# A gated unit's products with the weights as the stationary operand, in a two-layer decoder trunk

## The chip, the cores and the metric

One core of one Trainium2 chip runs the whole program. The metric is the device time of one execution in microseconds, the median of three runs; lower is better.

## What is computed

Two layers on 256 tokens of 2048 features, all in float32. In each layer one input projection of the normalised stream gives seven parts of 2048 columns; the change concerns two of them, `glu_a` and `glu_b`.

```python
h = rms_norm(x, norm_g[layer])                        # x (1, 256, 2048)
proj = jnp.einsum("bsd,de->bse", h, w_in[layer])      # w_in (2048, 14336)
q, k, v, g_att, glu_a, glu_b, g_conv = jnp.split(proj, SPLIT_POINTS, axis=-1)
...
u = glu_a * jax.nn.sigmoid(glu_b)
u = jnp.pad(u, ((0, 0), (CONV_WIDTH - 1, 0), (0, 0)))
y = lax.conv_general_dilated(u, dw_kernel[:, None, :], window_strides=(1,), padding="VALID",
        dimension_numbers=("NWC", "WIO", "NWC"), feature_group_count=D_CONV) + dw_bias
y = jax.nn.silu(layer_norm(y, ln_g, ln_b))
conv = jnp.einsum("bsc,ce->bse", y, w_pw)
...
y = jnp.einsum("bse,ed->bsd", jnp.concatenate([att_y, conv_y], axis=-1), w_out[layer])
x = x + y
```

The depthwise convolution is 31 taps wide and causal over the tokens. The rest of a layer is attention of 16 heads, SiLU gates and two more normalisations.

## The kernel before, in words

**Large products.** The weights come as tiles of 256 rows by 512 columns (`raw`, four buffers). ACT rounds each to float32r (`whi`, L227), DVE takes the rest (`wlo`, L228), and the operand, the transposed activations, is held as such a pair too: `st_hi`, `st_lo`, 128 features by 256 tokens for each of 16 contraction tiles. A product of float32 accuracy is three products of float32r: hi by hi (L629), hi by lo (L630) and lo by hi (L631). A *step* is one weight tile: two contraction tiles by two halves of the tokens by three, 12 products. In each the 128 tokens of a half are the stationary operand, loaded ahead of it (engine PEld), and 512 columns of the weights are streamed. A *group* is eight steps: one chunk of 512 columns of one part, summed in two PSUM banks (`acc`), one for each half of the tokens. There are 80 groups, 640 steps, counted from 0. Per layer the groups go glu_b, glu_a, v, q, k for each of the four chunks j, then g_conv and g_att, and then o_att, pw and o_conv, four chunks each. Splits of weight tiles stand three steps ahead of their products in the program (`AHEAD`).

**Everything else** is put between the steps by `Filler`: a task is a generator that yields what its next slice needs (`Need`: engine times, PSUM banks, a condition), and a slice is put into the program once an estimate of how far each engine has got says that it fits. Each engine then works in program order. The last step of a group adds the task that takes its sums (`users`).

**The tasks of the gated unit.** The operand is not scaled by the tokens' rms; `rx`, a factor per token, comes in when the sums are taken, where tokens are on the partitions, so that it is a scale per partition.

- `ev_glu_b` (L292): ACT writes sigmoid(sums x rx) to `Dt[0]`, one instruction per half of the tokens (L295).
- `ev_glu_a` (L298): DVE multiplies sums by rx and by `Dt[0]` (L301). Then PE transposes the result by 128x128 blocks, eight of them, into two PSUM banks (`transposes`, L249 to L255), and ACT copies them to `uT`, features on the partitions (L309).
- `conv` (L314) works on `uT` on DVE, 124 instructions per chunk, followed by `layer_norm`, `ln_square` and `ln_silu`. The latter needs a factor per token along the free dimension: GpSimd spreads `rstd` to `rbc`, PE multiplies it by the identity (L380) and ACT copies it to `nmean` (L382). A plain f32 product has two records in the trace, one for each of its passes.

`x_square` (L281) computes `rx` from squares of the stream and sets the flag that `ev_glu_b` waits for in the first chunk.

Of the kernel before, what the change touches and what calls it, by code (L numbers as in the profile page):

```python
# [13 lines left out]
AF = mybir.ActivationFunctionType  # L14
ALU = mybir.AluOpType
# [8 lines left out]
NCH = 4  # L24
CH = 512
EPS = 1e-6
# Columns of the per-feature parameters: the taps by layer, then pairs by layer.
P_BIAS, P_LNG, P_LNB, P_ATT, P_CONV = (DEPTH * CW + DEPTH * i for i in range(5))
NPRM = DEPTH * (CW + 5)

# Weight tiles of [128, KS, CH]: a step is the products of one of them.
KS = 2
NSTEP = KT // KS
R_RAW, R_SPLIT = 4, 4
AHEAD = 3


class Need:
    """What the next slice of a task takes: time by engine (us, in the order in which its operations follow
    from one another), PSUM banks, and a condition that has to hold first."""  # L40

    def __init__(self, banks=0, when=None, **time):
        self.banks, self.when, self.time = banks, when, list(time.items())
# [3 lines left out]


class Filler:
    """Work beside the large products, in slices between their steps.  # L50

    A task is a generator that yields the Need of its next slice. The engines work in program order, so a
    slice is put into the program where its operands will about have been computed, by an estimate of how
    far each engine has got, and not where it would make the splits of the next weight tiles late."""

    HOP = 0.2

# [29 lines left out]
            self.banks.append((b, self.now[4]))  # L87

    def use(self, time, ready):
        """The time at which operations that follow from one another end, the first not before ready."""  # L90
        start = end = ready
        for e, cost in time:
            start = max(self.t[e], start)
            end = max(start + cost, end + 0.3)
            self.t[e] = end
            if e == "G":  # shares VectorE's port
                self.t["V"] = max(self.t["V"], start) + cost
                end += 1.0
            start += 0.45
        return end + self.HOP  # L100
# [43 lines left out]
def trunk(ctx: ExitStack, tc: tile.TileContext, x, norm_g, w_in, q_norm_g, k_norm_g, dw_kernel, dw_bias,  # L144
# [8 lines left out]
    def t(shape, name, dt=F32):  # L153
        return sb.tile(shape, dt, name=name)

    # Stationary operands by chunk of four contraction tiles, as exact sums hi + lo of float32r.
    st_hi = [[t([128, 4, SEQ], f"sthi{s}{c}", F32R) for c in range(4)] for s in range(2)]
    st_lo = [[t([128, 4, SEQ], f"stlo{s}{c}", F32R) for c in range(4)] for s in range(2)]
    Y = [t([128, 4 * SEQ], f"y{c}") for c in range(4)]
# [30 lines left out]
    sm_m = [t([128, 2], f"smm{i}") for i in range(4)]  # L190
    sm_r = [t([128, 2], f"smr{i}") for i in range(4)]
    rbc = t([128, 2, 128], "rbc")

    acc = [pp.tile([128, CH], F32, name=f"acc{i}") for i in range(4)]
    fill = Filler([pp.tile([128, CH], F32, name=f"ax{i}") for i in range(4)], dict(V=4.5, A=3.5), 5)

    xs = [dr.tile([SEQ, CH], F32, name=f"xs{c}") for c in range(NCH)]

# [1 line left out]
    groups = []  # L200
    for l in range(DEPTH):
        for j in range(NCH):
# [26 lines left out]
        halved[i] = fill.use([("A", 0.95), ("V", 1.14)], loaded[i])  # L229
        load(i + R_RAW)  # L230

# [1 line left out]
    ready = [[False] * 4 for _ in range(2)]  # a chunk of the operand is in place  # L233
    vacant = [[True] * 4 for _ in range(2)]  # all its products are in the program
    flags = set()

    def flag(*what):
        flags.add(what)

    def has(*what):  # L240
        return lambda: what in flags

    def rsqrt(r, ss, scale, n):
        """r = (ss * scale + EPS) ** -0.5 on [128, n]"""
        G.tensor_scalar(r, ss, scale, EPS, op0=ALU.mult, op1=ALU.add)
        G.tensor_tensor(r, r, half[:, :n], op=ALU.pow)

    def transposes(src, banks):
        """[128 tokens, 2, 4 x 128] -> two banks of [128, 2, 256 tokens]"""  # L249
        for b in range(2):  # L250
            for i in range(2):
                for tt in range(2):
                    e = (2 * b + i) * 128
                    T.transpose(banks[b][:, i * SEQ + tt * 128:i * SEQ + tt * 128 + 128],  # L254
                                src[:, tt, e:e + 128], ident)  # L255

    def to_stationary(src, s, c, gain):
        """Transposes a chunk and splits it, times a gain per feature."""
        yield Need(2, lambda: vacant[s][c], P=0.9)
        banks = [fill.bank(), fill.bank()]  # L260
        transposes(src, banks)
        yield Need(A=1.5, V=1.6)
        p = [b[:, i * SEQ:(i + 1) * SEQ] for b in banks for i in range(2)]
        for i in range(4):
            S.activation(st_hi[s][c][:, i], p[i], AF.Copy, scale=gain(i))  # L265
        for i in range(4):
            V.scalar_tensor_tensor(st_lo[s][c][:, i], p[i], gain(i), st_hi[s][c][:, i].bitcast(F32),  # L267
                                   op0=ALU.mult, op1=ALU.subtract)
        fill.free(*banks)
        filled(s, c)  # L270
# [3 lines left out]
        ready[s][c] = True  # L274

    def x_chunk(l, c):
        """A chunk of the residual stream, in A, becomes the next layer's operand."""
        yield from to_stationary(A[c], 0, c, lambda i: ng[:, l * KT + 4 * c + i:l * KT + 4 * c + i + 1])
        fill.add(x_square(l, c), 3, fill.now[4])

    def x_square(l, c):  # L281
        yield Need(A=1.4)
        for tt in range(2):
            S.activation(junk, A[c][:, tt], AF.Square, accum_out=ssx[:, tt, c:c + 1])  # L284
        flag("x", l, c)
        if all(("x", l, k) in flags for k in range(4)):
            yield Need(V=0.1, G=0.6)
            V.tensor_reduce(rsc, ssx, axis=mybir.AxisListType.X, op=ALU.add)
            rsqrt(rx, rsc, 1.0 / D, 2)
            flag("rx", l)  # L290

    def ev_glu_b(l, j, ps):  # L292
        yield Need(0, has("glu", l, j - 1) if j else has("rx", l), A=1.2)
        for tt in range(2):
            S.activation(Dt[0][:, tt], ps[tt], AF.Sigmoid, scale=rx[:, tt:tt + 1])  # L295
        flag("ev", l, "glu_b", j)

    def ev_glu_a(l, j, ps):  # L298
        yield Need(0, has("ev", l, "glu_b", j), V=1.4)
        for tt in range(2):  # L300
            V.scalar_tensor_tensor(Dt[0][:, tt], ps[tt], rx[:, tt:tt + 1], Dt[0][:, tt],  # L301
                                   op0=ALU.mult, op1=ALU.mult)
        flag("ev", l, "glu_a", j)
        yield Need(2, has("conv", l, j - 2) if j >= 2 else None, P=0.9)
        banks = [fill.bank(), fill.bank()]
        transposes(Dt[0], banks)
        yield Need(A=1.0)
        for b in range(2):
            S.activation(uT[j % 2][:, 2 * b:2 * b + 2, PAD:], banks[b].rearrange("p (c s) -> p c s", c=2), AF.Copy)  # L309
        fill.free(*banks)  # L310
        flag("glu", l, j)
        fill.add(conv(l, j), 5 + j, fill.now[4])

# [229 lines left out]
            yield from x_chunk(l + 1, j)  # L543
            nc.sync.dma_start(xs[j].rearrange("(t p) e -> p t e", p=128), A[j])

# [1 line left out]
    ng_in = t2[:DEPTH * KT, :128]  # L547
    S.dma_start(ng_in, norm_g.rearrange("l (k p) -> (l k) p", p=128))
    make_identity(nc, ident)
# [54 lines left out]
    fill.add(parameters(), 1, 45.0)  # L604
    split(0)

# [1 line left out]
    users = {"glu_b": ev_glu_b, "glu_a": ev_glu_a, "v": ev_v, "g_conv": ev_g_conv, "g_att": ev_g_att,  # L608
             "pw": ev_pw, "o_att": ev_o_att, "o_conv": ev_o_conv,
             "q": lambda l, j, ps: ev_qk(l, j, ps, "q"), "k": lambda l, j, ps: ev_qk(l, j, ps, "k")}  # L610
# [1 line left out]
    for i, (g, s) in enumerate(tiles):  # L612
        l, nm, j, _, _, _, st = groups[g]
        c = s * KS // 4
        fill.until(lambda: ready[st][c])
        if s == 0 and g >= 2:
            fill.until(has("ev", *groups[g - 2][:3]))
        for a in range(i + AHEAD if i else 1, i + AHEAD + 1):
            split(a)
        ps = [acc[(2 * g + tt) % 4] for tt in range(2)]  # L620
        hi, lo = whi[i % R_SPLIT], wlo[i % R_SPLIT]
        order = [(kk, tt) for kk in range(KS) for tt in range(2)]
        if s == NSTEP - 1:
            order.sort(key=lambda o: o[1])
        for kk, tt in order:
            k = s * KS + kk
            tok = slice(tt * 128, tt * 128 + 128)
            xh, xl = st_hi[st][c][:, k % 4, tok], st_lo[st][c][:, k % 4, tok]
            T.matmul(ps[tt], xh, hi[:, kk], start=(k == 0), stop=False)  # L629
            T.matmul(ps[tt], xh, lo[:, kk], start=False, stop=False)  # L630
            T.matmul(ps[tt], xl, hi[:, kk], start=False, stop=(k == KT - 1))  # L631
        fill.use([("P", 2.6)], halved[i])
        if i >= 2 and later:
            nc.sync.dma_start(*later.pop(0))
        if i == NSTEP:
            G.dma_start(mask, log_count)
            rope_tables(0)
        if s % 2 and j == NCH - 1 and nm in last[st]:
            ready[st][c], vacant[st][c] = False, True
        if s == NSTEP - 1:  # L640
            fill.add(users[nm](l, j, ps), 0, fill.t["P"])
            if nm == "o_att" and j == NCH - 1 and l + 1 < DEPTH:
                rope_tables(l + 1)
        fill.run()
# [8 lines left out]


def log_counts():
    """By query (in its tile of 128) and key: the log of how many branches attend it."""
    q = np.arange(SEQ)[:, None]
    k = np.arange(SEQ)[None, :]
    d = q - k
# [28 lines left out]
```

## Time and profile before

| | |
|---|---|
| median of 3 runs | 1864.1 us (1863.65 to 1865.67) |
| profiled execution, first to last instruction | 1863.1 us |
| PE busy | 1849.6 us (99%), 8525 matmuls |
| PEld busy | 1541.2 us (83%) |
| DVE busy | 1394.8 us (75%) |
| ACT busy | 988.8 us (53%) |
| POOL busy | 136.3 us (7%) |
| chain that ended last | PE 97%, DMA 2% |
| granted TensorE clock, mean | 0.998 |

The span is the profiled execution's time by its instructions; the runs' times also hold what lies around it, 1.0 us at the median. PE's busy time holds the fill of the array, so that products overlap in it: the start of one to the start of the next tells more than a length.

### The profile page before, as it was taken

What the parts mean: (1) busy time and instruction counts of PE and PEld (TensorE: products, weight loads), DVE (VectorE), ACT (ScalarE), POOL (GpSimd) and SP (SyncE); (2) the same over time, 40 slices, a digit from 0 to 9 for tenths busy, and PEclk for the clock granted to TensorE, in tenths of its full rate; (3) what the DMA queues carried; (4) which work ended last, traced back from release to release, by engine and by line L of the source; (5) the groups of instructions that cost most, each with busy time, mean ns of one, the idle gap of its engine ahead of it and who ended that gap; (6) DMA issues with size and microseconds to landing.
All of it is one profiled execution on the core that took longest, in us unless ns stands there. A gap on an engine that the chain in (4) does not pass through costs nothing.

```text
span 1863.1 us, 23820 instructions
## 1 busy us (share of the span) xinstructions
PE 1849.6 (99%) x8525; PEld 1541.2 (83%) x8525; DVE 1394.8 (75%) x2160; ACT 988.8 (53%) x1559; POOL 136.3 (7%) x153
## 2 busy tenths in 40 slices
PE   8999999999999999999999999999999999999999
PEld 6888888888888888888888888888888888888887
DVE  4778889888889885556558888797887998755554
ACT  5465564564654464445444655646556445644542
POOL 1110100100110140000000101002000102100000
PEclk9999999999999999999999999999999999999999
DMA  7765656656566676666666656566565666666564
GB/s 237 204 184 167 180 180 180 182 168 190 174 180 193 177 231 210 192 190 190 208 203 192 188 161 184 159 199 183 160 185 165 194 195 190 213 204 195 178 205 145
DMA packets 180880, 349.98 MB, mean 188 GB/s; under 512 B 11064, under 2 KB 11096, under 8 KB 180760
## 3 DMA queue, kind: packets, MB, share of 16 engines
q1 hardware_dynamic: 179176, 345.61, 61.2%
q0 software_dynamic: 960, 1.77, 0.5%
q8 instruction: 67, 1.10, 0.2%
q10 hardware_dynamic: 624, 1.07, 0.2%
q14 instruction: 53, 0.43, 0.1%
HBM read 344.21 MB, written 4.19 MB: 187 GB/s over the span
## 4 chain that ended last, share of the span: by engine, by line
PE 97%; DMA 2%; ACT 0%; SPq 0%; DVE 0%; issue 0%; ACTq 0%; DVEq 0%
PE acc L630 31%; PE acc L631 31%; PE acc L629 31%; PE ax L254 2%; DMA raw<-in_w_in 2%; PE ax L452 1%; PE ax L469 1%; PE ax L478 0%; PE ax L477 0%; PE ax L476 0%; PE ax L451 0%; ACT whi L227 0%; DVE wlo L228 0%; SPq L551 0%; ACT junk L284 0%
## 5 line engine op out<-in xcount | busy, mean ns | idle before, releaser
L228 DVE TENSOR_TENSOR wlo<-raw,whi 128x1024 fp32r<-128x1024 f32 x640 | 792.2, 1246 | 404.5 <-ACT whi L227 400.4
L227 ACT ACTIVATE whi<-raw 128x1024 fp32r<-128x1024 f32 x640 | 675.3, 1063 | 671.1 <-PE acc L631 471.5
L629 PE MATMUL acc<-whi,sthi 128*128 128x512 f32 x2560 | 1005.9, 393 | 2.7 <-ACT whi L227 2.7
L630 PE MATMUL acc<-wlo,sthi 128*128 128x512 f32 x2560 | 998.1, 390 | 0.8 <-DVE wlo L228 0.8
L631 PE MATMUL acc<-whi,stlo 128*128 128x512 f32 x2560 | 998.3, 390 | 0.0
L629 PEld LDWEIGHTS acc<-whi,sthi 128*128 128x128 f32 x2560 | 481.7, 188 | 100.9 <-ACT whi L227 3.1
L631 PEld LDWEIGHTS acc<-whi,stlo 128*128 128x128 f32 x2560 | 481.5, 188 | 101.0
L630 PEld LDWEIGHTS acc<-wlo,sthi 128*128 128x128 f32 x2560 | 481.8, 188 | 98.8 <-DVE wlo L228 1.1
L326 DVE SCALAR_TENSOR_TENSOR y<-ut,prm,y 128x256 f32<-128x256 f32 x960 | 411.1, 486 | 0.0
L414 POOL TENSOR_SCALAR qr<-qss 128x8 f32<-128x8 f32 x16 | 3.2, 197 | 692.1 <-ACT junk L411 692.1
L411 ACT ACTIVATE junk<-acc,rx 128x128 bf16<-128x128 f32 x128 | 47.1, 368 | 8.4 <-PE acc L631 4.8
L334 POOL TENSOR_TENSOR ysum<-ysum,y 128x256 f32<-128x256 f32 x30 | 31.8, 1058 | 237.1 <-DVE y L326 235.7
L421 ACT ACTIVATE d<-acc,qr 128x128 f32<-128x128 f32 x128 | 34.8, 383 | 18.0 <-POOL qr L416 18.0
L265 ACT ACTIVATE sthi<-ax,prm 128x256 fp32r<-128x256 f32 x64 | 25.1, 475 | 31.1 <-PE ax L254 31.1
L267 DVE SCALAR_TENSOR_TENSOR stlo<-ax,prm,sthi 128x256 fp32r<-128x256 f32 x64 | 26.5, 475 | 15.8 <-ACT sthi L265 15.8
L442 ACT ACTIVATE c<-ax 128x512 f32<-128x512 f32 x32 | 17.4, 597 | 33.6 <-PE ax L254 33.6
L465 ACT ACTIVATE sm<-sm,smm 128x128 f32<-128x128 f32 x64 | 28.2, 443 | 6.6 <-DVE smm L460 6.6
L362 POOL TENSOR_TENSOR ssum<-ssum,d 128x512 f32<-128x512 f32 x14 | 26.8, 1912 | 5.9 <-ACT d L355 5.0
L415 POOL TENSOR_TENSOR qr<-qr,half 128x8 f32<-128x8 f32 x16 | 26.3, 1642 | 1.3
L254 PEld LDWEIGHTS ax<-ident,d 128*128 128x128 f32 x192 | 22.4, 140 | 3.2
L254 PE MATMUL ax<-ident,d 128*128 128x128 f32 x192 | 24.9, 273 | 0.0
L411 ACT ACTIVATION_READ_ACCUMULATOR junk<-acc,rx 128x1 f32 x128 | 24.7, 193 | 0.0
(106 smaller groups left out, 669.4 us busy)
## 6 DMA issues: line engine op xcount, KB each, us to landing
raw<-in_w_in SPq DMA_DIRECT2D x448, 512.0 KB, 3.9
raw<-in_w_out SPq DMA_DIRECT2D x128, 512.0 KB, 4.6
raw<-in_w_pw SPq DMA_DIRECT2D x64, 512.0 KB, 4.6
a<-in_x SPq DMA_DIRECT2D x8, 512.0 KB, 5.7
xs<-a SPq DMA_DIRECT2D x4, 512.0 KB, 6.0
a<-xs SPq DMA_DIRECT2D x4, 512.0 KB, 6.5
out<-a SPq DMA_DIRECT2D x4, 256.0 KB
out<-a ACTq DMA_DIRECT2D x4, 256.0 KB, 5.1
```

The source lines that it names most:

```text
L227: S.activation(hi, a, AF.Copy)
L228: V.tensor_sub(wlo[i % R_SPLIT], a, hi.bitcast(F32))
L254: T.transpose(banks[b][:, i * SEQ + tt * 128:i * SEQ + tt * 128 + 128], src[:, tt, e:e + 128], ident)
L326: V.scalar_tensor_tensor(y[:, c], u[:, c, k:k + SEQ], w[:, c, l * CW + k:l * CW + k + 1], y[:, c], op0=ALU.mult, op1=ALU.add)
L334: G.tensor_add(ysum, ysum, y[:, c])
L362: G.tensor_add(ssum, ssum, half_sq)
L411: S.activation(junk[:, :DH], ps[tt][:, h * DH:(h + 1) * DH], AF.Square, scale=rx[:, tt:tt + 1], accum_out=qss[:, tt, h:h + 1])
L421: S.activation(n[:, tt, h * DH:(h + 1) * DH], ps[tt][:, h * DH:(h + 1) * DH], AF.Copy, scale=qr[:, tt, h:h + 1])
L465: S.activation(s[:, cs], s[:, cs], AF.Exp, bias=m[:, tt:tt + 1], scale=-1.0, accum_out=lsum[:, tt:tt + 1])
L629: T.matmul(ps[tt], xh, hi[:, kk], start=(k == 0), stop=False)
L630: T.matmul(ps[tt], xh, lo[:, kk], start=False, stop=False)
L631: T.matmul(ps[tt], xl, hi[:, kk], start=False, stop=(k == KT - 1))
```

## The change

In the groups of glu_b and glu_a the operands change places. A block of 128x128 weights is the stationary operand and all 256 tokens are streamed, so that a step has two contraction tiles by four blocks of features by three, 24 products of 256 columns. The sums have features on the partitions; a bank holds two blocks of 256 tokens. The factor `rx` now lies along the free dimension, so `x_square` makes `rxb` of it, spread over all partitions, by a copy on GpSimd, two products with the identity and a copy on ACT; `rxb` uses the buffer of `nmean`. `ev_glu_b` multiplies by `rxb` on DVE and takes the sigmoid on ACT in one instruction of 1024 columns; `ev_glu_a` multiplies sums by the gate, and then by `rxb` straight into `uT`. The transposes and their copies go. Other groups are as before.

```diff
     rbc = t([128, 2, 128], "rbc")
+    rxb = nmean
...
             rsqrt(rx, rsc, 1.0 / D, 2)
             flag("rx", l)
+            G.tensor_copy(rbc, rx[:, :, None].to_broadcast([128, 2, 128]))
+            yield Need(1, P=0.5)
+            ps = fill.bank()
+            for tt in range(2):
+                T.matmul(ps[:, tt * 128:tt * 128 + 128], rbc[:, tt], ident, start=True, stop=True)
+            yield Need(A=0.4)
+            S.activation(rxb, ps[:, :SEQ], AF.Copy)
+            fill.free(ps)
+            flag("rxb", l)
...
     def ev_glu_b(l, j, ps):
-        yield Need(0, has("glu", l, j - 1) if j else has("rx", l), A=1.2)
-        for tt in range(2):
-            S.activation(Dt[0][:, tt], ps[tt], AF.Sigmoid, scale=rx[:, tt:tt + 1])
+        yield Need(0, has("glu", l, j - 1) if j else has("rxb", l), V=1.4)
+        d = Dt[0].rearrange("p t (i s) -> p t i s", i=2)
+        for b in range(2):
+            V.tensor_mul(d[:, b], ps[b].rearrange("p (i s) -> p i s", i=2), rxb[:, None, :].to_broadcast([128, 2, SEQ]))
         flag("ev", l, "glu_b", j)
+        yield Need(A=1.1)
+        S.activation(Dt[0], Dt[0], AF.Sigmoid)
+        flag("sig", l, j)
 
     def ev_glu_a(l, j, ps):
-        yield Need(0, has("ev", l, "glu_b", j), V=1.4)
-        for tt in range(2):
-            V.scalar_tensor_tensor(Dt[0][:, tt], ps[tt], rx[:, tt:tt + 1], Dt[0][:, tt],
-                                   op0=ALU.mult, op1=ALU.mult)
+        yield Need(0, has("sig", l, j), V=1.4)
+        for b in range(2):
+            V.tensor_mul(Dt[0][:, b], ps[b], Dt[0][:, b])
         flag("ev", l, "glu_a", j)
-        yield Need(2, has("conv", l, j - 2) if j >= 2 else None, P=0.9)
-        banks = [fill.bank(), fill.bank()]
-        transposes(Dt[0], banks)
-        yield Need(A=1.0)
-        for b in range(2):
-            S.activation(uT[j % 2][:, 2 * b:2 * b + 2, PAD:], banks[b].rearrange("p (c s) -> p c s", c=2), AF.Copy)
-        fill.free(*banks)
+        yield Need(0, has("conv", l, j - 2) if j >= 2 else None, V=1.25)
+        V.tensor_mul(uT[j % 2][:, :, PAD:], Dt[0].rearrange("p t (i s) -> p (t i) s", i=2),
+                     rxb[:, None, :].to_broadcast([128, 4, SEQ]))
...
+        if nm in FEATURE_MAJOR:
+
+            order = [(kk, f) for kk in range(KS) for f in range(4)]
+            if s == NSTEP - 1:
+                order.sort(key=lambda o: o[1] // 2)
+            for kk, f in order:
+                k = s * KS + kk
+                fs = slice(f * 128, f * 128 + 128)
+                o = ps[f // 2][:, f % 2 * SEQ:f % 2 * SEQ + SEQ]
+                xh, xl = st_hi[st][c][:, k % 4], st_lo[st][c][:, k % 4]
+                first = k == 0 and f % 2 == 0
+                T.matmul(o, hi[:, kk, fs], xh, start=first, stop=False, skip_group_check=True)
+                T.matmul(o, lo[:, kk, fs], xh, start=False, stop=False, skip_group_check=True)
+                T.matmul(o, hi[:, kk, fs], xl, start=False, stop=(k == KT - 1), skip_group_check=True)
+        else:
...
```

`FEATURE_MAJOR` is ("glu_b", "glu_a"); under `else` stand the products as they were. Lines of the changed program are its own: L645 to L647 are the products of the gated unit's groups there, L656 to L658 those of the others, L231 the split on DVE, L309, L318 and L321 the three steps of the gated unit on DVE, L312 the sigmoid.

Three places show the order of instructions. First PE, in the first step of the first group, one contraction tile of the program before (`acc` is the PSUM bank, the number behind a name its buffer):

```order
L629 MATMUL acc0_153<-whi0_93,sthi00_65 128x512
L630 MATMUL acc0_153<-wlo0_97,sthi00_65 128x512
L631 MATMUL acc0_153<-whi0_93,stlo00_73 128x512
L629 MATMUL acc1_154<-whi0_93,sthi00_65 128x512
L630 MATMUL acc1_154<-wlo0_97,sthi00_65 128x512
L631 MATMUL acc1_154<-whi0_93,stlo00_73 128x512
```

and in the changed program, from the second block of features of the first bank to the first block of the second bank:

```order
L645 MATMUL acc0_153<-sthi00_65,whi0_93 128x256
L646 MATMUL acc0_153<-sthi00_65,wlo0_97 128x256
L647 MATMUL acc0_153<-stlo00_73,whi0_93 128x256
L645 MATMUL acc1_154<-sthi00_65,whi0_93 128x256
L646 MATMUL acc1_154<-sthi00_65,wlo0_97 128x256
L647 MATMUL acc1_154<-stlo00_73,whi0_93 128x256
```

Where three products of 512 columns filled a bank's share of a contraction tile, three of 256 now fill half of it, and three more like them, for the bank's other block of features, stand beside them: twelve instead of six in all.

Second PE, in the group of v of the second chunk, around the transposes of the gated unit's result (`d0`), before:

```order
L630 MATMUL acc3_156<-wlo0_97,sthi00_65 128x512
L631 MATMUL acc3_156<-whi0_93,stlo00_73 128x512
L254 MATMUL ax2_159<-ident_116,d0_107 128x128 x4
L254 MATMUL ax3_160<-ident_116,d0_107 128x128 x4
L629 MATMUL acc2_155<-whi1_94,sthi00_65 128x512
```

and in the changed program:

```order
L657 MATMUL acc3_156<-wlo0_97,sthi00_65 128x512
L658 MATMUL acc3_156<-whi0_93,stlo00_73 128x512
L656 MATMUL acc2_155<-whi1_94,sthi00_65 128x512
L657 MATMUL acc2_155<-wlo1_98,sthi00_65 128x512
L658 MATMUL acc2_155<-whi1_94,stlo00_73 128x512
```

The eight transposes are gone and the next step follows directly.

Third DVE, where the sums of glu_a of the second chunk are taken (`acc0`, `acc1`), between splits of weight tiles and taps of the first chunk's convolution, before:

```order
L228 TENSOR_TENSOR wlo2_99<-raw2_91,whi2_95 128x1024
L301 SCALAR_TENSOR_TENSOR d0_107<-acc0_153,rx_133,d0_107 128x512
L301 SCALAR_TENSOR_TENSOR d0_107<-acc1_154,rx_133,d0_107 128x512
L228 TENSOR_TENSOR wlo3_100<-raw3_92,whi3_96 128x1024
L326 SCALAR_TENSOR_TENSOR y0_81<-ut0_101,prm_124,y0_81 128x256 x4
```

and in the changed program:

```order
L231 TENSOR_TENSOR wlo2_99<-raw2_91,whi2_95 128x1024
L318 TENSOR_TENSOR d0_107<-acc0_153,d0_107 128x512
L318 TENSOR_TENSOR d0_107<-acc1_154,d0_107 128x512
L321 TENSOR_TENSOR ut1_102<-d0_107,nmean_126 128x4x256
L231 TENSOR_TENSOR wlo3_100<-raw3_92,whi3_96 128x1024
```

One instruction of 1024 columns stands ahead of the next split that did not stand there before; two more (L309) stand at the end of each glu_b group. On DVE the last split of the layer norm's result in the first layer stands behind the split of weight tile 248, before it stood behind that of tile 236; the first group of pw begins with tile 256.

## Rows read from the trace of the kernel before

**Rows 1.** The page: span, and busy time of the engines.
```profile
span 1863.1 us, 23820 instructions
...
PE 1849.6 (99%) x8525; PEld 1541.2 (83%) x8525; DVE 1394.8 (75%) x2160; ACT 988.8 (53%) x1559; POOL 136.3 (7%) x153
```

**Rows 2.** The page: the chain that ended last, share of the span by engine.
```profile
PE 97%; DMA 2%; ACT 0%; SPq 0%; DVE 0%; issue 0%; ACTq 0%; DVEq 0%
```

**Rows 3.** Groups by line and shape, PE: xcount | busy us, mean ns.
```profile
L629 PE MATMUL acc<-whi,sthi 128*128 128x512 f32 x2560 | 1005.9, 393 | 2.7 <-ACT whi L227 2.7
```

**Rows 4.** Stretches of one group: length, busy PE, PEld, DVE, ACT, POOL, clock, DMA, GB/s.
```profile
34.34:63.79 29.45, 26.04 (x109) 20.70 (x108) 12.80 (x12) 12.23 (x13) 9.54 (x17) 0.88 0.76 214
...
205.09:226.85 21.76, 21.76 (x98) 18.02 (x96) 18.57 (x29) 10.16 (x14) 1.66 (x2) 1.00 0.66 192
...
300.67:323.33 22.66, 22.66 (x106) 18.85 (x104) 21.04 (x37) 10.17 (x11) 0.00 (x0) 1.00 0.66 193
```

**Rows 5.** PE in order of time, steady: start us, length us, engine, line, instruction.
```profile
1637.41 0.39 PE L629 MATMUL acc<-whi,sthi 128*128 128x512 f32 x1
...
1640.13 0.39 PE L629 MATMUL acc<-whi,sthi 128*128 128x512 f32 x1
```

**Rows 6.** PE in order of time, plain f32 products of attention.
```profile
151.21 0.38 PE L451 MATMUL ax<-c,c 128*128 128x128 f32 x2
151.43 0.60 PE L452 MATMUL ax<-c,c 128*128 128x256 f32 x2
151.86 0.38 PE L451 MATMUL ax<-c,c 128*128 128x128 f32 x2
```

**Rows 7.** PEld in order of time: loads beside two-column matmuls, then a large product's.
```profile
674.28 1.08 PEld L370 LDWEIGHTS ax<-ones,ssum 128*128 128x128 f32 x8
675.28 0.19 PEld L629 LDWEIGHTS acc<-whi,sthi 128*128 128x128 f32 x1
675.39 0.19 PEld L630 LDWEIGHTS acc<-wlo,sthi 128*128 128x128 f32 x1
```

**Rows 8.** PE in order of time, the nine products after twelve transposes (L469).
```profile
158.13 0.40 PE L630 MATMUL acc<-wlo,sthi 128*128 128x512 f32 x1
...
160.22 0.39 PE L630 MATMUL acc<-wlo,sthi 128*128 128x512 f32 x1
```

**Rows 9.** PE in order of time around its wait at 42 us.
```profile
42.28 0.39 PE L631 MATMUL acc<-whi,stlo 128*128 128x512 f32 x1
45.31 0.50 PE L629 MATMUL acc<-whi,sthi 128*128 128x512 f32 x1 [2.65 <-ACT whi L227]
46.58 0.79 PE L630 MATMUL acc<-wlo,sthi 128*128 128x512 f32 x1 [0.76 <-DVE wlo L228]
...
47.59 0.63 PE L629 MATMUL acc<-whi,sthi 128*128 128x512 f32 x1
...
51.43 0.63 PE L629 MATMUL acc<-whi,sthi 128*128 128x512 f32 x1
```

**Rows 10.** Two stretches of one us, columns as in rows 4.
```profile
7.00:8.00 1.00, 0.28 (x3) 0.06 (x1) 0.30 (x1) 1.00 (x3) 0.00 (x0) 1.00 1.05 408
...
49.00:50.00 1.00, 1.00 (x4) 0.81 (x3) 0.47 (x1) 0.99 (x1) 0.12 (x1) 0.50 1.08 307
```

**Rows 11.** PE in order of time: four passes of the broadcast of the layer norm.
```profile
683.34 0.40 PE L631 MATMUL acc<-whi,stlo 128*128 128x512 f32 x1
683.57 0.61 PE L380 MATMUL ax<-ident,rbc 128*128 128x128 f32 x4
...
684.25 0.39 PE L630 MATMUL acc<-wlo,sthi 128*128 128x512 f32 x1
```

**Rows 12.** Groups by line and shape, DVE and ACT.
```profile
L301 DVE SCALAR_TENSOR_TENSOR d<-acc,rx,d 128x512 f32<-128x512 f32 x16 | 11.3, 744 | 0.2 <-PE acc L631 0.2
...
L390 DVE TENSOR_TENSOR y<-y,nmean 128x1024 f32<-128x1024 f32 x8 | 9.4, 1219 | 0.0
...
L309 ACT ACTIVATE ut<-ax 128x512 f32<-128x512 f32 x16 | 8.7, 596 | 17.3 <-PE ax L254 17.3
```

More of the change, by code (lines that the diff above doesn't have):

```diff
@@ L35 @@
 AHEAD = 3
+FEATURE_MAJOR = ("glu_b", "glu_a")
 class Need:
@@ L621, in trunk @@
         hi, lo = whi[i % R_SPLIT], wlo[i % R_SPLIT]
[L622 to L631, printed above, removed]
+        if nm in FEATURE_MAJOR:
[12 more added lines that the diff above has]
+        else:
+            order = [(kk, tt) for kk in range(KS) for tt in range(2)]
+            if s == NSTEP - 1:
+                order.sort(key=lambda o: o[1])
+            for kk, tt in order:
+                k = s * KS + kk
+                tok = slice(tt * 128, tt * 128 + 128)
+                xh, xl = st_hi[st][c][:, k % 4, tok], st_lo[st][c][:, k % 4, tok]
+                T.matmul(ps[tt], xh, hi[:, kk], start=(k == 0), stop=False)
+                T.matmul(ps[tt], xh, lo[:, kk], start=False, stop=False)
+                T.matmul(ps[tt], xl, hi[:, kk], start=False, stop=(k == KT - 1))
         fill.use([("P", 2.6)], halved[i])
```

## The prediction

> **What bounds the kernel now.** I read the page first, then the chain of waits, then the stretches of single groups, and last the instructions of TensorE in order of time. The page has PE busy for 1849.6 of 1863.1 us [rows 1], and the chain is PE for 97% of the span [rows 2]. A stretch of one group shows why: 96 large products take 21.76 us with nothing between them, and at most 18.6 us of DVE and 10.2 of ACT lie beside them [rows 4]. So what PE issues is the time, and every ns of a large product's pitch counts: there are 3 x 2560 of them [rows 3]. PE's one real wait is near the start, at 42 us [rows 9], where a weight tile comes late; outside it, work on other engines costs nothing unless PE is made to wait for it.
>
> The mean of 393 ns [rows 3] is a length with the fill of the array in it. What counts is the pitch: twelve products from one L629 to the next take 2.72 us, 226.7 ns each [rows 5].
>
> **The change part by part.** *Large products.* In 16 of the 80 groups (two of the gated unit, four chunks, two layers) a step's 12 products of 512 moving columns become 24 of 256, each with its own load of 128x128. That is 128 steps, 1536 products at 226.7 ns = 348.2 us before and 3072 products at a pitch p after. The columns streamed are as many as before; the loads are twice as many. No large product in the trace has 256 columns, so p has to be bounded.
>
> From below: beside matmuls of two columns the loads are all that is left. The eight loads of L370 and the next take 1.00 us, of which the first waits 0.227 for a large product; (1.00 - 0.227)/7 = 0.110, and the next two loads, of large products, are 0.11 apart [rows 7]. So p is at least 111 ns, however well loads hide; now a load of 111 hides under 227.
>
> What 256 columns take themselves: after the wait at 42 us PE ran at the granted clock 0.50 [rows 10], the level of 1.2 GHz, and nine products took 3.84 us, 426.7 each [rows 9], which is 512 columns at 1.2 GHz and nothing else. At 2.4 GHz the same would be 213.3, but the pitch is 226.7: 13.3 ns are added that the slower array does not show. Plain f32 products, which take twice the time per column, show 215 for 256 columns and 110 for 128 [rows 6], so 2 to 3 ns. The 13.3 ns thus belong to feeding the array at full rate. If they go with the columns, 256 of them take 113.3. If they go with each product and its load, they take 106.7 + 13.3 = 120.0. I take 120.0, because the extra is not a steady rate: behind a run of transposes nine products take 2.09 us, 232.2 each [rows 8], 18.9 over the array's 213.3, until the old pitch returns. An excess that depends on how the loads stand to the products looks like load and stream disturbing each other, and each product still has one load. The upper end is the undisturbed array plus that larger excess, 106.7 + 18.9 = 125.6.
>
> The Trainium skill, "TensorE: Matmul & The Clock Gate", Part 2, step 1, speaks for the change here: TensorE has two independent read ports, and loading the next weights steals nothing from the running stream; its section on the back-to-back gap gives N/2.4 + 2.5 ns, which is 215.8 for 512 columns and 109.2 for 256. The trace has 226.7 where that gives 215.8, so for these operands it disagrees. By the page the loads of 111 would set the pitch, and this term would be a gain of 7.2 us.
>
> At p = 120.0: 3072 x 0.120 = 368.6, so **+20.5 us**. Ends: 341.0 (-7.2) and 385.8 (+37.6).
>
> *Transposes.* Eight blocks of eight transposes go away, since the sums already have features on the partitions. Such a block stands in a group of v, 22.66 against 21.76 us [rows 4]: 0.90 each, **-7.2 us**. Their eviction on ACT, two of 596 ns each [rows 12], was beside.
>
> *Broadcast of the norm.* Per layer GpSimd copies rx to rbc, PE multiplies it by the identity, ACT copies it out. The layer norm does the same on L380: from the product ahead to the one behind 0.91 us where two pitches are 0.45 [rows 11], so 0.46 each, **+0.9 us**. It stands behind the first group, when rx is long there.
>
> *The wait at the start.* PE stands from the last product of step 10 (42.28) to 45.31, and then 0.76 us more for the low half; the tile was late from memory [rows 9], its load being released by ACT and DVE, not by PE. What PE does slower ahead of that point shortens the wait: 11 steps x (24 x 0.120 - 2.72 = 0.16) + 0.46 = **-2.2 us**. The clock fell behind this wait, and some 14 products up to 52.7 us ran at 426.7 instead of 226.7. An idle of 0.7 us in a stretch with PE busy 0.28 near the start left the clock at 1.00 [rows 10]. With the first idle cut to about half a us, I expect the clock to stay: 14 x 0.200 = **-2.8 us**. If it falls all the same, that term is 0.
>
> *DVE and ACT.* Per chunk the two L301 (0.744) become four products with PSUM and one of 1024 columns (1.219) [rows 12]: 4 x 0.744 + 1.219 - 1.488 = 2.7 us more on DVE, 22 us in all; ACT loses two evictions. The sigmoid now waits for DVE, and behind it in ACT's queue stand splits of weight tiles; these are three steps ahead of PE, 8.2 us, and DVE's two products and the sigmoid are under 4. In the new order the layer norm's last split comes 12 weight tiles later on DVE than before, still ahead of the tile that needs it. DVE had 21.0 of 22.7 us busy in a middle stretch [rows 4], but that includes the convolution, which is put where there is room. I cost this at nothing; the cover is those three tiles and, for the convolution, the eight tiles from the last split (tile 248) to the first group of pw (tile 256).
>
> Sum: 20.5 - 7.2 + 0.9 - 2.2 - 2.8 = +9.2, so a span of 1872.3. The runs' median of 1864.1 lies 1.0 above the span, which I add: **1873.3 us**. A measurement can tell about 0.2%, 3.7 us.
>
> **The rivals.** *Columns carry the excess, or loads alone set the pitch.* The place is the same stream. At p = 113.3 the first term is 0, the wait is shortened by 0.5 only, the clock falls as before, and the span changes by -7.2 + 0.9 - 0.5 = -6.8: 1857.3. At p = 111 it is 7.2 less, about 1850; this is what the Trainium skill's page named above leads to. The case decides against my forecast below p = 116 or so. For it: the pitch settles at exactly 17/16 of the array's time, which a feed with a fixed rate could give. Against: 232.2 behind transposes [rows 8]. Chances 0.16 and 0.06.
>
> *Load and stream slow each other both.* Now loads fill half of the stream's time; with p = 120 they would fill nearly all of it. If a load of 111 is itself stretched by 18.9, p = 130: 399.4, +51.2 and, with the other terms (the wait then shortened by all of its 3.4), about 1903. For it: rows 8 show that phases matter. Against: at the settled pitch the load leaves room. Chance 0.08.
>
> *DVE makes PE wait.* If all 22 us came to the path, about 1895. The cover above speaks against it: 0.03.
>
> *The change does not do what it says.* The order shows 24 products per step and no transposes there: excluded.
>
> **How the numbers follow.** Forecast 0.67, of which 0.07 with p between 114 and 117.5 lies within 0.2%. Faster: 0.16 + 0.06 = 0.22. Within: 0.07 and a little of the first rival's upper side, 0.09. Slower: the rest, 0.69. The forecast's own range: p = 117 gives about +0.2, p = 125.6 gives 37.6 - 7.2 + 0.9 - 3.4 - 2.8 = +25.1, so 1865 to 1890. The range reaches down to 1857 to hold the column case; it leaves out loads alone (0.06), p of 130 (0.08), and a few per cent above: 1857 to 1890.
>
> **What would show it.** The steps of the gated unit's groups at 2.88 us instead of 2.72, with products 120 ns apart; a group of the gated unit without other work at 23.0 us instead of 21.8; groups of v at 21.8; the stretch from 34 to 64 us with the clock near 1.00 and a wait under 1 us ahead of the first product; DVE near 1416 us and no wait of PE in the rest. The prediction is wrong if the pitch is 113 or less, or over 126, or if PE waits for DVE or ACT in the middle.

## The result, and the profile after

The changed kernel takes 1876.2 us (median of 4 runs, 1875.1 to 1878.7) against 1864.35 (4 runs): a ratio of 1.0065, 95% interval 1.0053 to 1.0077, 11.9 us more. The forecast was 1873.3, slower, within 1857 to 1890.

The page of the changed kernel answers to [rows 1, 2]:

```profile
span 1874.9 us, 26793 instructions
...
PE 1862.2 (99%) x10005; PEld 1616.6 (86%) x10005; DVE 1419.9 (76%) x2184; ACT 981.4 (52%) x1537; POOL 144.6 (8%) x155
...
PE 97%; DMA 2%; ACT 0%; DVE 0%; SPq 0%; issue 0%; ACTq 0%; DVEq 0%
```

PE is still busy for 99% of the span and 97% of the chain. Its instructions have grown from 8525 to 10005: 1536 products more, 64 transposes fewer, 8 passes of the broadcast more. The answer to [rows 5] is in order of time on PE; 24 products lie between these two rows:

```profile
1062.03 0.28 PE L645 MATMUL acc<-sthi,whi 128*128 128x256 f32 x1
...
1064.91 0.28 PE L645 MATMUL acc<-sthi,whi 128*128 128x256 f32 x1
```

2.88 us for 24 products is 120.0 ns each, the value that the prediction took, and a step of the gated unit's groups costs 2.88 us instead of 2.72. The stretches of groups answer to [rows 4]; they are, in order, the second group of the program, the first group of the third chunk, a group of glu_a with nothing between its products, and the group of v behind it (columns as there):

```profile
36.52:65.55 29.03, 26.36 (x208) 25.56 (x206) 13.86 (x14) 11.47 (x13) 8.63 (x13) 0.94 0.70 202
251.92:279.66 27.74, 27.74 (x230) 27.53 (x228) 20.71 (x45) 19.19 (x49) 3.08 (x3) 1.00 0.53 163
...
970.27:993.32 23.05, 23.05 (x195) 23.05 (x194) 11.07 (x11) 10.70 (x10) 0.00 (x0) 1.00 0.64 184
993.32:1015.10 21.78, 21.78 (x98) 18.02 (x97) 20.10 (x34) 9.18 (x9) 0.00 (x0) 1.00 0.65 190
```

The undisturbed group has gone from 21.76 to 23.05 us, with PEld busy from end to end; the group of v from 22.66 to 21.78, since its transposes are gone. The first group of the third chunk, with attention between its products, takes 27.74 us, 1.2 more rather than 1.28; its row of before:

```profile
249.51:276.06 26.55, 26.55 (x133) 22.44 (x132) 20.52 (x45) 19.40 (x48) 3.08 (x3) 1.00 0.53 169
```

The second group has 29.03 us where [rows 4] have 29.45, with a mean clock of 0.94 for 0.88.

What PE waited for, longest in total, after the loads of the first 8 us (which are as before): line, releaser, us in total, times, longest:

```profile
PE ax L596 <- DMA y<-in_conv_out_g: 1.6, 1, 1.6
PE acc L646 <- DVE wlo L231: 1.1, 2, 0.9
```

The two waits for the weight tile, 2.65 and 0.76 us [rows 9], have become one of 0.9 in the same place, and a new one of 1.6 has come up behind it, for the last row of the per-feature parameters, which PE transposes at L596. In order of time on PE:

```profile
46.68 0.39 PE L646 MATMUL acc<-sthi,wlo 128*128 128x256 f32 x1 [0.88 <-DVE wlo L231]
...
58.50 0.28 PE L647 MATMUL acc<-stlo,whi 128*128 128x256 f32 x1
60.36 0.60 PE L596 MATMUL ax<-ident,y 72*128 72x72 f32 x6 [1.58 <-DMA y<-in_conv_out_g]
...
61.27 0.42 PE L645 MATMUL acc<-sthi,whi 128*128 128x256 f32 x1
...
63.19 0.41 PE L645 MATMUL acc<-sthi,whi 128*128 128x256 f32 x1
```

From the first of the last two rows to the second, nine products take 1.92 us, 213 ns each: 256 columns at the half clock, 213.3, and again no excess. The clock had fallen behind the new wait, for 3.4 us (columns as in [rows 4]):

```profile
61.10:64.40 3.30, 3.30 (x18) 3.30 (x17) 2.32 (x3) 0.10 (x1) 1.51 (x3) 0.50 0.94 250
```

That is the profiled execution. Two of the four have a mean granted clock of 1.000, which leaves no room for 3.4 us at the half level; they took 1875.1 and 1875.7 us.

### The profile page after: what moved, and what is told of

Read it like the earlier page. It is cut to its first block, busy times and chain, and to the rows that moved or that the text cites. A ratio compares the mean times of both kernels' runs of the same rounds, so it can differ in the third digit from the quotient of the medians.

```text
span 1874.9 us, 26793 instructions
## 1 busy us (share of the span) xinstructions
PE 1862.2 (99%) x10005; PEld 1616.6 (86%) x10005; DVE 1419.9 (76%) x2184; ACT 981.4 (52%) x1537; POOL 144.6 (8%) x155
## 3 DMA queue, kind: packets, MB, share of 16 engines
q8 instruction: 78, 1.28, 0.3%
## 4 chain that ended last, share of the span: by engine, by line
PE 97%; DMA 2%; ACT 0%; DVE 0%; SPq 0%; issue 0%; ACTq 0%; DVEq 0%
PE acc L656 25%; PE acc L657 25%; PE acc L658 25%; PE acc L647 6%; PE acc L645 6%; PE acc L646 6%; DMA raw<-in_w_in 2%; PE ax L257 2%; PE ax L464 1%; PE ax L481 1%; PE ax L489 0%; PE ax L490 0%; PE ax L488 0%; PE ax L463 0%; DMA y<-in_conv_out_g 0%; DVE wlo L231 0%
## 5 line engine op out<-in xcount | busy, mean ns | idle before, releaser
L231 DVE TENSOR_TENSOR wlo<-raw,whi 128x1024 fp32r<-128x1024 f32 x640 | 794.6, 1250 | 377.6 <-ACT whi L230 373.7
L656 PE MATMUL acc<-whi,sthi 128*128 128x512 f32 x2048 | 801.1, 391 | 0.0
L658 PE MATMUL acc<-whi,stlo 128*128 128x512 f32 x2048 | 797.3, 389 | 0.0
L657 PE MATMUL acc<-wlo,sthi 128*128 128x512 f32 x2048 | 797.1, 389 | 0.0
L658 PEld LDWEIGHTS acc<-whi,stlo 128*128 128x128 f32 x2048 | 384.4, 188 | 80.2
L656 PEld LDWEIGHTS acc<-whi,sthi 128*128 128x128 f32 x2048 | 384.6, 188 | 78.5
L657 PEld LDWEIGHTS acc<-wlo,sthi 128*128 128x128 f32 x2048 | 384.6, 188 | 78.1
L645 PE MATMUL acc<-sthi,whi 128*128 128x256 f32 x1024 | 294.4, 287 | 0.0
L646 PE MATMUL acc<-sthi,wlo 128*128 128x256 f32 x1024 | 291.2, 284 | 1.1 <-DVE wlo L231 1.1
L647 PE MATMUL acc<-stlo,whi 128*128 128x256 f32 x1024 | 291.1, 284 | 0.0
L646 PEld LDWEIGHTS acc<-sthi,wlo 128*128 128x128 f32 x1024 | 197.9, 193 | 1.9 <-DVE wlo L231 1.5
L645 PEld LDWEIGHTS acc<-sthi,whi 128*128 128x128 f32 x1024 | 197.9, 193 | 0.7 <-ACT whi L230 0.2
L647 PEld LDWEIGHTS acc<-stlo,whi 128*128 128x128 f32 x1024 | 197.7, 193 | 0.0
```

Of the source, the lines that this page charges most:

```text
L231: V.tensor_sub(wlo[i % R_SPLIT], a, hi.bitcast(F32))
L645: T.matmul(o, hi[:, kk, fs], xh, start=first, stop=False, skip_group_check=True)
L646: T.matmul(o, lo[:, kk, fs], xh, start=False, stop=False, skip_group_check=True)
L647: T.matmul(o, hi[:, kk, fs], xl, start=False, stop=(k == KT - 1), skip_group_check=True)
```

## Experiments

### Where the 13.3 ns come from

The prediction's 120.0 rested on a choice: that the excess over the array's own time goes with each product and not with its columns. The kernel before was given other shapes in some groups of v and k, with this in the place of the three products of a step:

```diff
+            N, M = FORM.get((l, nm, j), (CH, 128))
+            tok = slice(tt * 128, tt * 128 + M)
             xh, xl = st_hi[st][c][:, k % 4, tok], st_lo[st][c][:, k % 4, tok]
-            T.matmul(ps[tt], xh, hi[:, kk], start=(k == 0), stop=False)
+            T.matmul(ps[tt][:M, :N], xh, hi[:, kk, :N], start=(k == 0), stop=False)
...
```

> The kernel before, with other shapes of its large products in the groups of v and k: fewer weight columns streamed, or fewer tokens loaded as the stationary operand. It leaves out those columns and tokens, so its output is not the trunk's and its time says nothing; read is the pitch inside a step at the full clock. Theory 1, the 13.3 ns belong to each load and go with the columns that it loads: pitch N/2.4 + 13.3 x M/128, not under 111 x M/128. So 448 columns with a full load 200.0, 384: 173.3, 320: 146.7, 256: 120.0, 128: 111; 512 columns with loads of 96, 64, 32 columns: 223.3, 220.0, 216.7; 256 with 64: 113.3. Theory 2, they belong to each product, whatever is loaded: the same for full loads, but 226.7 for 512 columns with any load, and 120.0 for 256 with 64. Theory 3, the excess goes with the streamed columns (17/16) and 120 ns is the pace of a full load beside such a stream: 448: 198.3, 384: 170.0, 320: 141.7, and 120 for 256, 192, 128 and 64; 256 with a load of 64: 113.3.

Two rows of each of four forms, in order of time on PE, twelve products apart: 384 columns with a full load; 512 with a load of 64; 256 with a load of 64; 128 with a full load:

```profile
302.63 0.33 PE L637 MATMUL acc<-whi,sthi 128*128 128x384 f32 x1
...
304.71 0.33 PE L637 MATMUL acc<-whi,sthi 128*128 128x384 f32 x1
...
342.43 0.40 PE L637 MATMUL acc<-whi,sthi 128*64 128x512 f32 x1
...
345.19 0.40 PE L637 MATMUL acc<-whi,sthi 128*64 128x512 f32 x1
...
1008.37 0.28 PE L637 MATMUL acc<-whi,sthi 128*64 128x256 f32 x1
...
1009.73 0.28 PE L637 MATMUL acc<-whi,sthi 128*64 128x256 f32 x1
...
1186.78 0.28 PE L637 MATMUL acc<-whi,sthi 128*128 128x128 f32 x1
...
1188.12 0.28 PE L637 MATMUL acc<-whi,sthi 128*128 128x128 f32 x1
```

Each of the four distances divided by twelve: 173.3, 230.0, 113.3 and 111.7 ns. The other widths with a full load, over the same twelve: 448 columns 202.7, 320 columns 146.7, 256 columns 120.0, 192 columns 111.7.

So theory 3 is out: 384 columns take 173.3 and not 170.0, and loads of 128 columns keep up at 111 beside a stream, so that 120 is no limit of theirs. With a full load the pitch is N/2.4 + 13.3, down to the point where the load's 111 takes over, near 235 columns (448 runs a little higher, 202.7 against 200.0, in a pattern that does not settle). The 235 is worked out from the two, no width between 192 and 256 was run. How the excess depends on the load is open: neither theory 1 nor theory 2 holds. A quarter or half of the load leaves 512 columns at 230 to 232 (theory 1: 216.7 to 220.0), but half a load takes 256 columns down to 113.3 (theory 2: 120.0). A quarter gives 256 columns 113.3 in some steps and 117.8 in others; 128 columns take 60.0 with half a load and with a quarter. With narrow loads the excess changes from one product to the next, by some 6 to 23 ns. As in [rows 8] it may depend on how loads and products stand to each other; no run shows it.

The second run asks whether it belongs to exchanging weights as such, or to operands of four bytes:

```diff
+            if kind == "bf":
+                ob = ones.bitcast(BF16)
+                mv = ob[:, None, :].to_broadcast([128, 2, 256]) if n == 512 else ob[:, :n]
+                for q in range(3):
+                    T.matmul(ps[tt][:, :n], ob[:, :128], mv, start=(k == 0 and q == 0), stop=(k == KT - 1 and q == 2))
+                continue
```

> The kernel before, with other operands in five groups: in the groups of v of the first layer's chunks 1, 2 and 3 the products take bfloat16 constants, 512, 256 and 128 columns with a full load each; in the groups of k of chunks 1 and 2 they take 64 and 32 of the 128 contraction rows, float32r, 512 columns. It leaves out what those groups compute, and its time says nothing; read is the pitch inside a step at the full clock. Theory, the excess is the price of reading four-byte operands at the full rate beside a load: bfloat16 shows 216 for 512 columns and 109 for 256, within 3 ns of the array's time, and fewer rows change nothing (226.7 or the unsettled 230). Rival, it is the price of exchanging the weights, whatever their type: 226.7 and 120 for bfloat16 as well.

Two merged rows of that run, in order of time on PE, 512 and 256 columns of bfloat16:

```profile
184.67 2.54 PE L642 MATMUL acc<-ones 128*128 128x512 bf16 x11
...
301.79 3.44 PE L642 MATMUL acc<-ones 128*128 128x256 bf16 x30
```

Less the length of the last one (0.38 and 0.27), ten starts take 2.16 us and 29 take 3.17: 216 and 109 ns, and 128 columns took 56, with a load ahead of each product. The Trainium skill ("TensorE: Matmul & The Clock Gate", Part 1, section "Wait — 56ns, not 53.3ns?") gives N/2.4 + 2.5 for products back to back, 215.7 and 55.6 ns at 512 and 128 columns. For bfloat16 the trace agrees with that, for float32r (226.7 at 512) it does not. So exchanging the weights does not cost 13.3 ns by itself. In these runs the excess goes with operands of four bytes at the full clock, but two more things differ: the loads of bfloat16 are shorter (98 ns long in the trace, against 188), and stream and load read one constant tile over and over. Which of the three decides was not separated. 64 of 128 rows change nothing, 226.7.

### The two halves of the change

> Only the products of the change (24 of 256 columns per step in the gated unit's groups); the evictions, the transposes and their copies stand as before, so tokens and features are mixed up in the gated unit and the output is not the trunk's. By the prediction's terms and the profile's pitch of 120.0: +20.5 us for the products, less what the waits of the first 66 us swallow (up to 5 us): 1880 to 1885. Rival, that part of the change's increase comes from the new evictions: at most what the change itself shows plus 7, and less of it the more they cost; under 1880.

```diff
+        if nm in FEATURE_MAJOR:
+            order = [(kk, f) for kk in range(KS) for f in range(4)]
...
+                T.matmul(o, hi[:, kk, fs], xh, start=first, stop=False, skip_group_check=True)
...
```

The products are those of the change; what takes the sums stands as in the kernel before.

It took 1881.5 us, ratio 1.0092 (1.0075 to 1.0109): 17.2 us more than the kernel before, within the 1880 to 1885 expected. Its profile has the waits of the start, but the clock stood at 1.00 from 12 us to the end of PE's work (mean clock, and waits of PE behind the first 8 us):

```profile
core 0: 1879.8 us, clock 1.000
...
PE ax L585 <- DMA y<-in_conv_out_g: 1.5, 1, 1.5
PE acc L634 <- ACT whi L228: 1.0, 1, 1.0
PE acc L635 <- DVE wlo L229: 0.9, 1, 0.9
```

The other half:

> Only the evictions of the change (broadcast of the norm factor, products on DVE, sigmoid on ACT, no transposes and no copies of them), with the large products as before, so that tokens and features are mixed up in the gated unit and the output is not the trunk's. By the prediction's terms: -7.2 for the transposes, +0.9 for the broadcast: -6.3, about 1858; the wait near the start as before. Rival, DVE's additional 22 us reach the path in part: above 1860, with waits of PE for DVE between 100 and 650 us.

```diff
-FEATURE_MAJOR = ("glu_b", "glu_a")
+FEATURE_MAJOR = ()
```

It took 1859.2 us, ratio 0.9970 (0.9958 to 0.9981): 5.1 less, where 6.3 were expected. 17.2 - 5.1 = 12.1, and the change measured 11.9, so the halves add up. Each half has a start of its own, though (in the second the clock fell for 3.4 us at 48 us), and the intervals are some 2 to 3 us wide on either side: a third part of that size is not excluded. The waits of PE in the second half, its first 8 us left out, all lie before 66 us:

```profile
PE acc L656 <- ACT whi L230: 2.0, 1, 2.0
PE ax L596 <- DMA y<-in_conv_out_g: 1.4, 1, 1.4
PE acc L657 <- DVE wlo L231: 0.8, 1, 0.8
```

DVE was busy for 1416 us there, 21 more than before, and made PE wait for 0.8 us in all, as before; the rival that put those 21 us on the path is out. The wait for the row (1.5 and 1.4 us) stands in both halves, and not in the kernel before.

### The start

The prediction let the change hide 2.2 us in the first wait and keep the clock up for another 2.8. In the profile the clock fell after all, elsewhere. Three runs test it. The first moves only the parameters' transposes:

```diff
-    fill.add(parameters(), 1, 45.0)
+    fill.add(parameters(), 1, 56.0)
```

> The changed kernel, with the sixteen transposes of the per-feature parameters about four steps later on PE (the planner's time from which they may go is 56 instead of 45), and nothing else. Theory: behind the change PE still waits at 60 us, for the last parameter row from memory (1.6 us), and its clock falls there (3.4 us at half level, 1.7 lost); with the transposes later both go: 1.6 + 1.7 = 3.3 us less than the changed kernel, about 1873, clock at 1.00 up to the end. Rival: the clock falls for the late weight tiles at 45 us, or the last row is as late as before: within 1 us of the changed kernel, about 1876.

It took 1874.2 us, ratio to the kernel before 1.0052 (1.0038 to 1.0065), 2.0 less than the changed kernel; the two intervals overlap. The wait for the row is gone, 1.6 us, but the clock fell all the same, at 47 us and for 3.4 us, behind what is left of the wait for the late tile:

```profile
PE acc L646 <- DVE wlo L231: 0.9, 1, 0.9
PE acc L645 <- ACT whi L230: 0.6, 1, 0.6
```

Half the theory and half the rival. The profiled execution is the slowest of the four; the other three have a mean clock of 1.000 and took 1873.7 to 1874.4, near the theory's 1873. How long PE waits does not by itself tell whether its clock falls: with 1.0 and 0.9 us in the same place it stayed up in the profile of the products alone. No run tells what decides. The other two take the small loads out of the way of the weights:

```diff
-    fill.add(parameters(), 1, 45.0)
+    fill.add(parameters(), 1, 78.0)
...
-        if i >= 2 and later:
+        if i >= 12 and later:
             nc.sync.dma_start(*later.pop(0))
-        if i == NSTEP:
+        if i == 3 * NSTEP:
             G.dma_start(mask, log_count)
```

> The kernel before, with the loads of the parameters (twelve small ones, from step 12 instead of 2 on), of the mask and of the rotary tables (from step 24 instead of 8) and the transposes of the parameters (from 78 instead of 45 in the planner's time) later. Theory: the weight tile at 42 us is late because those loads share the queues with it; without them PE's wait of 3.4 us goes, and the half clock behind it, 2.8 us: about 1858. Rival: the weight stream is late of its own accord at the start: about 1864. The convolution starts some 30 us later; if its slack did not hold, PE would wait ahead of pw and the time would rise.

> The changed kernel with the same later loads and transposes. Theory: its waits of 0.9, 0.2 and 1.6 us in the first 66 us and the half clock (1.7 us) go, about 1872; then the difference to the kernel before with the same start is what the products, transposes and broadcast make by themselves: 14.2 us by the prediction's terms (20.5 - 7.2 + 0.9). Rival: the difference stays at 12, as between the two kernels, because the start did not count.

The kernel before took 1858.6 us with it, ratio 0.9968 (0.9956 to 0.9980): 5.8 less, clock at 1.00 to the end. All that PE waited for behind the first 8 us:

```profile
PE acc L630 <- DVE wlo L228: 0.6, 1, 0.6
```

So the tile at 42 us was late for small loads that had been put around it, and the wait with the half clock behind it cost about 6 us, as worked out. The edit moves two sets of loads and the transposes at once. The transposes stood at 60 us before, behind the wait, so they had not made the tile late; which of the loads weighs most wasn't tried. This version beats both kernels.

The changed kernel took 1874.1 us with it, ratio 1.0051 (1.0038 to 1.0063), clock at 1.00 too. That is 2.1 less than without (the intervals overlap), not 4.4, for PE met a wait that had not been there:

```profile
PE acc L658 <- DVE stlo L409: 1.4, 1, 1.4
PE acc L657 <- DVE wlo L231: 0.8, 1, 0.8
```

The 1.4 us lie at 762 us, at the start of pw: the low half of the layer norm's result (L409) comes too late from DVE. The convolution begins 28 us later in both versions; the kernel before takes that without a wait, the changed one, with 25 us more work on DVE, does not. The cover that the prediction named, the stretch from the layer norm's last split to pw, is some 23 us in the changed kernel (22 by the prediction's eight tiles), and a start 28 us later uses it up. Without this wait the two spans, 1858.2 and 1872.5, differ by 12.9 us, and the two medians, 1858.6 and 1874.1, by 14.1; the prediction's terms for products, transposes and broadcast were 14.2. The profiled execution of the kernel before is the slowest of its six, which makes the difference of the spans too small; the medians, 14.1, are the better way and agree with the terms. The rival (12, the start does not count) lies 2 us below; the intervals of the two ratios, some 2.3 us on either side, do not exclude it.

## Why the prediction was right, point by point

- **Products, +20.5 forecast.** The pitch is 120.0 ns, and an undisturbed group costs 1.28 us more, as forecast. The value was right; its reason, load and stream disturbing each other, stays open: a narrower load makes 256 columns faster and 512 slower. Groups with attention or other work between their products cost 1.17 to 1.18 more, not 1.28: before, products behind an interruption run at up to 236 ns, 232.2 in the mean of nine [rows 8]; in the changed kernel the products of 256 columns behind one run at 112 to 125. Over the 14 groups behind the first two that is 16.7 us, without the broadcast of the second layer, where the forecast had 17.9.
- **Transposes, -7.2 forecast.** 0.87 us each in the groups of v, 7.0 in all. Right.
- **Broadcast, +0.9.** The first group of the second layer has 24.33 us for 22.65: 1.28 and 0.40. Right.
- **The start, -5.0 forecast.** This is the step that failed, "I expect the clock to stay". The row that it leaned on was read wrongly. The clock 1.00 at 7 us [rows 10] is not a clock that an idle had left up: the first large products behind it in the kernel before, of 512 columns, start 0.43 us apart, which is the half level, up to 11.8 us. The trace has no record of the clock ahead of that, and the view prints 1.00 there.

```profile
10.14 0.63 PE L630 MATMUL acc<-wlo,sthi 128*128 128x512 f32 x1
10.57 0.63 PE L631 MATMUL acc<-whi,stlo 128*128 128x512 f32 x1
10.99 0.63 PE L629 MATMUL acc<-whi,sthi 128*128 128x512 f32 x1
```

  The first two groups took 54.2 us before and 55.8 after, +1.6, where the terms had 2 x 1.28 + 0.46 - 2.2 - 2.8 = -2.0. The wait for the tile did shrink, from 3.4 to 0.9, and the clock stayed up behind it. So PE came early to the next thing: its last product ahead of the parameters' transposes began at 58.50, and the first half of their last row, which SP issues between weight tiles, landed only at 60.3 (from the chain of waits: start us, us, what):

```profile
54.34 5.97 DMA y<-in_conv_out_g
```

  Before, PE had reached the first of these transposes (L584) only at 60.28, after its stretch at the half clock, and waited for nothing. The row was also later itself: before, issued at 54.44, it gave its last signal of landing at 58.5. Had it kept that, PE would have met no wait. In the changed kernel SP had issued four weight tiles between 50.0 and 53.9 us, before, between 48.0 and 54.0; that the row stood behind more of them is likely, not shown. The wait of 1.6 us and 16 products at 213 ns instead of 120 behind it, 1.5 us, are 3.1 of the 3.6 by which this term is off. The prediction had asked what slower products hide in the wait that the trace showed, and not what is late next. The term's 2.8 for the clock was too large besides: in the two executions of the changed kernel whose clock stayed up, the time was still some 2 us above the forecast, and the two executions of the kernel before with a mean clock of 1.000 took 1863.0 and 1863.8, about 1 us less than the median, not 2.8. The spans differ by 11.8 where 9.2 were forecast, 2.6 more: these 3.6, less the 1.2 by which interrupted groups were cheaper than forecast, and some tenths. That the forecast came within 2.9 us is in part luck, since the two misses have opposite signs.
- **DVE at nothing.** Busy time rose by 25 us, 22 were forecast. The new lines answer to [rows 12]; they take 30.9 us where L301 took 11.3, and the rest of the rise is older lines that take a little longer:

```profile
L318 DVE TENSOR_TENSOR d<-acc,d 128x512 f32<-128x512 f32 x16 | 10.8, 688 | 2.0 <-PE acc L647 2.0
...
L309 DVE TENSOR_TENSOR d<-acc,nmean 128x512 f32<-128x512 f32 x16 | 10.3, 683 | 0.0
...
L321 DVE TENSOR_TENSOR ut<-d,nmean 128x1024 f32<-128x1024 f32 x8 | 9.8, 1225 | 0.3
```

  PE waited for none of it in the changed kernel behind the first 66 us. With a later start it did, for 1.4 us.
- **The rivals.** Columns carrying the excess: the changed kernel's 120.0 and the 173.3 for 384 columns exclude it. Loads alone: right as a floor, at 111 to 112, but only below 235 columns. Load and stream stretching each other to 130: not seen, 256 columns settle at 120.0. The Trainium skill's rule that loading takes nothing from the stream ("TensorE: Matmul & The Clock Gate", Part 2, step 1) agrees with bfloat16 here. For float32r each product has 13.3 ns more, so the gain of 7.2 us did not come; whether the load takes them is not shown, since no run streamed float32r without a load.

## What to carry to other kernels

Swapping the operands to get results ready transposed doubled the number of loads here and halved the columns behind each: price such a swap by the pitch of the narrower product (here N/2.4 + 13.3 ns for float32r, with a floor of 111 for the load) against the transposes that it saves (here 0.9 us for eight), and only then look at the other engines. Where the sign hangs on a few ns per product, look in the trace for stretches in which the excess is larger, or absent, before choosing whether it goes with columns or with products. Where slower work hides in an early wait, ask which transfer is late next, and check a printed clock against the pitch of the products beside it; small loads issued among the tiles of a stream can make a tile late (moving them gave 5.8 us here).

## What was not expected of the hardware

- The excess of float32r products is not there at the lower clock: 512 columns take 426.7 ns and 256 take 213, which is the array's time at 1.2 GHz.
- In the run with fewer contraction rows, products of 64 rows ran at the full clock, while the group of 32 rows fell to half, with PE busy throughout and nothing waited for. Two stretches of that run, 64 rows and 32 rows (columns as in [rows 4]):

```profile
230.00:245.00 15.00, 15.00 (x70) 11.95 (x70) 14.21 (x24) 7.97 (x15) 0.00 (x0) 1.00 0.68 210
341.00:351.00 10.00, 10.00 (x24) 7.58 (x24) 9.82 (x13) 4.60 (x11) 5.41 (x6) 0.50 0.48 155
```

  The pitch there was 426.7 ns. No run tells why.
- A narrower load makes 512 columns slower: 230 to 232 ns with loads of 32 to 96 columns, against 226.7 with 128, and the pitch from one product to the next then keeps changing.
